# Eighteen spinning matmuls in three array shapes instead of twenty-six in one, ahead of a PE-bound encoder block

## The chip, the cores and the metric

The kernel runs on one core of one Trainium2 chip. The metric is device time in microseconds (us) of that core for one launch; lower is better. A core has five engines that run side by side and meet at semaphores: TensorE (PE, with its weight loads shown apart as PEld), VectorE (DVE), ScalarE (ACT), GpSimd (POOL) and SyncE (SP, which here only issues DMAs).

## The reference, cut to what matters

One encoder layer on 1024 tokens of width 1024: a projection, two kinds of attention, a gate, a second projection and a layer norm.

```python
h = jnp.einsum('bsd,de->bse', x, w_in[layer])
q_a, k_a, v_a, z_a, q_b, k_b, v_b, z_b = jnp.split(h, SPLIT_POINTS, axis=-1)
y_a = neighborhood_attention(q_a, k_a, v_a, rel_pos_bias[layer])      # 8 heads, 8 x 16 windows on a 16 x 64 grid
y_b = windowed_gqa_with_sink(rotary(q_b), rotary(k_b), v_b, sink_logits[layer])   # 8 heads, 2 key heads, |i-j| <= 128
mixed = jnp.concatenate([y_a * silu(z_a), y_b * silu(z_b)], axis=-1)
y = jnp.einsum('bse,ed->bsd', mixed, w_out[layer])
x = layer_norm(DEEPNORM_ALPHA * x + y, ln_gain[layer], ln_bias[layer])
```

None of this involves the spinning matmuls: they multiply zeros by zeros and nobody reads their result.

## The kernel before, in words

Precision is kept by splitting each float32 operand into a high and a low part and doing three matmuls (high by high, low by high, high by low) for each product. The kernel has these stages, in this order on PE:

1. **The spin** (line 412). A tile `warm` of 128 x 128 f16 zeros is written by DVE (line 127), and 26 matmuls multiply it by itself into one PSUM bank with the tag "t".
2. **The V projection, first half of the tokens** (`v_mms`, line 486). For each of eight slices k of the inner dimension there are 24 matmuls of 128 x 128 by 128 x 320: four token tiles, two column halves, three passes, in fp32r. For slice k the raw weights `wvraw` (DMA issued in line 435 or 457) become `wvh` on ACT (line 442, or 463 for the first slice) and `wvl` on DVE (line 445, or 466), and the raw tokens `xraw` (DMA in line 423 or 458) become `x` high (ACT, line 426, or DVE, line 464, for the first slice) and `x` low (line 429 or 465). The first matmul needs the first halves of `wvh` and of `x` high.
3. **The V projection, second half**, from f16 parts (line 486 again), which need scales worked out from all of x and wv.
4. **The combined projection** (`project`, line 379): 21 column tiles, with 16 x 3 matmuls of 128 x 512 each. From column tile 6 on, its matmuls are dealt out between those of the attention units (lines 816, 817, 881, 901).
5. **The output projection and the layer norm** (line 1031 and `final`), which end with the row tile 7 (lines 1104 to 1118).

The order of each engine's instructions is settled when the kernel is built, by a scheduler that runs the program against a timeline; inside `tc.manual_schedule()` it is the order of the text. DMAs of the first stages sit on SP's queue in the order in which the text issues them.

Tiles come from pools. `const` holds small tiles for the whole kernel; `vw` holds those of the V projection; the PSUM tag "t" has two banks that are handed out in turn.

The spin as it stands:

```python
warm = const.tile([128, 128], F16, name="warm")      # line 126
nc.vector.memset(warm, 0.0)
...
ps = bank("t")
for _ in range(26):
    nc.tensor.matmul(ps[:, :128], warm, warm, start=True, stop=True)     # line 412
```

Of the kernel before, what the change touches and what calls it, by code (L numbers as in the profile page):

```python
# [9 lines left out]
F16 = mybir.dt.float16  # L10
# [51 lines left out]
def hybrid_block(ctx, tc, xT, x, wt, wv, wo, bias, sink, gain, lbias, cos, sin, bmask, out):  # L62
    nc = tc.nc
    PS = bass.MemoryType.PSUM

    const = ctx.enter_context(tc.tile_pool(name="const", bufs=1))
# [7 lines left out]
    def bank(tag):  # L74
        bufs = {"pj": 2, "s": 4, "t": 2}[tag]
        return (ps1 if bufs == 1 else ps2).tile([128, 512], F32, tag=tag, name=f"ps_{tag}", bufs=bufs)
# [6 lines left out]
    def big_tile(name, shape=(128, 2, 512), dt=F32R):  # L83
        n = taken[0]
        taken[0] += 1
        tag = "big" if n < 8 or 16 <= n < 24 or n >= 32 + NS else "big2"
        return big.tile(list(shape), dt, tag=tag, name=name)

    xh, xl, x16h, x16l = {}, {}, {}, {}
    for half in range(2):  # L90
        for k in range(KT):
            t = big_tile(f"x{half}{k}", dt=F32 if half else F32R)
# [30 lines left out]
    sg = const.tile([128, 3], F32, name="sg")  # L123
    rsg = const.tile([128, 1], F32, name="rsg")
    junk = zp.tile([128, 2048], BF16, tag="ze", name="junk", bufs=1)
    warm = const.tile([128, 128], F16, name="warm")
    nc.vector.memset(warm, 0.0)
    ones = const.tile([128, 128], BF16, name="ones")
    nc.vector.memset(ones, 2.0 ** -13)
    bm = const.tile([128, 384], F32, name="bm")  # L130
    sk = const.tile([128, 8], F32, name="sk")
    nsk = const.tile([128, 8], F32, name="nsk")
# [272 lines left out]
    with ExitStack() as vctx:  # L405
        vp = vctx.enter_context(tc.tile_pool(name="vp", bufs=2))
        vw = vctx.enter_context(tc.tile_pool(name="vw", bufs=1))
        wvh, wvl = [], []
        wvm = vw.tile([128, KT], F32, name="wvm")
        ps = bank("t")  # L410
        for _ in range(26):
            nc.tensor.matmul(ps[:, :128], warm, warm, start=True, stop=True)  # L412

        wraw, xraw, nst = {}, {}, [0]

# [230 lines left out]
        for a in range(2):  # L646
            ps = bank(tags[4 + a])
# [211 lines left out]
    def quad(q):  # L859
        g, p, j, t, _ = units[4 * q]  # L860
        return g, p, j, t // 4 if g == "b" else t[0] // 2
# [319 lines left out]
    for i in range(-LD, NU + LO):  # L1181
# [38 lines left out]
        q, m = divmod(i - LP - 3, 4)  # L1220
        if i >= Q30 + 2:
            q, m = (NU // 4 - 2, i - Q30 - 2) if i < Q30 + 4 else divmod(i - LP - 3, 4)
        elif i >= Q30:
            q, m = -1, 0
# [10 lines left out]
        if 0 <= q < NU // 4:  # L1235
            g, p, j, h = quad(q)
# [88 lines left out]
```

## Time and profile before

| what | value |
|---|---|
| runs | 446.01, 446.91, 447.51 us; median 446.91 us |
| span of the profiled execution (first to last instruction) | 444.7 us |
| time of the profiled execution as a run | not listed; the runs lie 1.3 to 2.8 us above its span |
| PE busy | 437.5 us (98%), 3289 matmuls |
| DVE, ACT, POOL busy | 344.2, 308.3, 221.6 us |
| spin | from 0.98 us, 26 matmuls, 2.96 us |
| first matmul of the V projection | 3.89 us |

How to read it: the span starts with the first instruction on any engine, so times within the trace count from there. A matmul's end is modelled, and matmuls overlap, so the pace of PE is read from the distance between the starts of neighbours and not from their durations. The granted clock (PEclk) is the share of full speed that the throttle allows TensorE, as far as the profile recorded it.

### The profile page before, as it was taken

The page shows a single profiled execution, that of the slowest core. Times are in us where ns is not written, and L with a number is a line of the kernel's source. Part 1 is how long each engine was busy: PE and PEld are TensorE (multiplying, and loading weights), DVE is VectorE, ACT ScalarE, POOL GpSimd, SP SyncE. Part 2 cuts the span into 40 slices and gives each one's busy share as a digit, 9 for nine tenths or more (in the row PEclk, how much of TensorE's full clock was granted, in tenths as well). Part 3 has the DMA queues.
Part 4 walks back from the last instruction along what each step waited for, and adds up shares of the span by engine and source line. Part 5 has one row for each costly group of instructions (what it writes and reads, how often), then busy time and mean ns, then how long its engine had stood idle before and what let it go on. Part 6 is the DMA issues. An engine that isn't in the chain of part 4 may idle for free.

```text
span 444.7 us, 9505 instructions
## 1 busy us (share of the span) xinstructions
PE 437.5 (98%) x3289; PEld 255.5 (57%) x3289; DVE 344.2 (77%) x849; ACT 308.3 (69%) x700; POOL 221.6 (50%) x235
## 2 busy tenths in 40 slices
PE   9999999999999999999999999999999999999994
PEld 8997754444445565655565655656555654444453
DVE  5978967438986898887988888888878837589944
ACT  5759789766499988887868887888778946302401
POOL 0110074646839558866506767765574405205740
PEclk9999999999999999999999999999999999999997
DMA  8921469984659999587978899998999998103612
GB/s 272 390 91 60 145 235 339 336 292 169 213 127 214 206 190 181 98 162 143 164 127 175 169 182 180 213 170 213 192 204 253 167 172 347 55 0 102 232 69 72
DMA packets 133841, 81.39 MB, mean 183 GB/s; under 512 B 101280, under 2 KB 113440, under 8 KB 133536
## 3 DMA queue, kind: packets, MB, share of 16 engines
q1 hardware_dynamic: 133648, 80.64, 75.4%
q8 instruction: 26, 0.43, 0.4%
q14 instruction: 23, 0.19, 0.2%
q10 hardware_dynamic: 144, 0.13, 0.1%
HBM read 50.34 MB, written 9.96 MB: 136 GB/s over the span
## 4 chain that ended last, share of the span: by engine, by line
PE 91%; DMA 3%; POOL 3%; DVE 1%; issue 1%; ACT 1%; SPq 0%; POOLq 0%; DVEq 0%; ACTq 0%
PE ps_pj L379 44%; PE ps_s L1031 9%; PE ps_s L486 6%; PE ps_t L881 6%; PE ps_pj L1031 5%; PE ps_t L1031 5%; PE ps_s L816 4%; PE ps_s L817 4%; PE ps_pj L486 3%; PE ps_t L486 3%; DMA bias<-in_bias 3%; PE ps_t L901 1%; POOL wl L205 1%; PE ps_t L412 1%; POOL ks L295 1%
## 5 line engine op out<-in xcount | busy, mean ns | idle before, releaser
L379 PE MATMUL ps_pj<-xf,wh 128*128 128x512 f16 x672 | 202.1, 379 | 0.1
L379 PE MATMUL ps_pj<-xf,wl 128*128 128x512 f16 x336 | 127.3, 379 | 0.0
L379 PEld LDWEIGHTS <-wh 128*128 128x128 f16 x672 | 63.7, 98 | 60.4 <-DVE ks L263 0.5
L842 ACT ACTIVATE ps_s<-sn,nm 128x385 f32<-128x385 f32 (+3 forms) x128 | 70.1, 548 | 25.1 <-DVE nm L826 24.6
L853 DVE SCALAR_TENSOR_TENSOR split<-ps_s,split 128x384 f16<-128x384 f32 (+2 forms) x128 | 65.7, 513 | 27.5 <-ACT split L852 25.9
L1031 PEld LDWEIGHTS <-m 128*128 128x128 f16 x432 | 40.0, 98 | 41.1 <-DVE m L939 0.2
L852 ACT ACTIVATE split<-ps_s 128x384 f16<-128x384 f32 (+2 forms) x128 | 57.8, 452 | 2.5 <-DMA tr<-split 0.2
L204 POOL TENSOR_SCALAR wr<-wr,wsc 128x512 f32<-128x512 f32 x26 | 20.6, 791 | 68.1 <-ACT wh L199 61.6
L379 PEld LDWEIGHTS <-wl 128*128 128x128 f16 x336 | 32.9, 98 | 37.4
L826 DVE CUSTOM_DVE_ANT_0 sn<-ps_s,bm,nsk 128x384 f32<-128x384 f32 (+1 forms) x64 | 40.7, 636 | 2.0 <-PE ps_s L817 1.7
L1031 PE MATMUL ps_s<-wo,m 128*128 128x512 f16 (+1 forms) x192 | 40.8, 366 | 0.0
L816 PE MATMUL ps_s<-ks,qs 128*128 128x384 f16 (+4 forms) x128 | 39.2, 306 | 0.3 <-DVE qs L263 0.3
L817 PE MATMUL ps_s<-ks,qs 128*128 128x384 f16 (+4 forms) x128 | 39.2, 306 | 0.0
L826 DVE CUSTOM_DVE_ANT_0 sn<-ps_s,bias,sg 128x264 f32<-128x264 f32 (+1 forms) x64 | 35.0, 547 | 4.5 <-issue 1.5
L881 PEld LDWEIGHTS <-tr 128*128 128x128 f16 (+1 forms) x1104 | 36.6, 98 | 2.2
L205 POOL TENSOR_TENSOR wl<-wr,wh 128x512 f16<-128x512 f32 x26 | 32.7, 1257 | 2.2
L788 POOL TENSOR_SCALAR bias<-bias,rsg 128x552 f32<-128x552 f32 (+1 forms) x24 | 19.1, 797 | 23.8 <-DMA bias<-in_bias 22.6
L295 POOL COPY ks<-ks 64x512 f16<-64x512 f16 x40 | 26.0, 661 | 7.1 <-DVE ks L263 2.8
L1086 ACT ACTIVATE sd<-mv,eps 128x1 f32<-128x1 f32 x8 | 2.4, 295 | 36.5 <-DVE mv L1084 35.2
L1031 PE MATMUL ps_pj<-wo,m 128*128 128x512 f16 (+1 forms) x144 | 26.2, 326 | 0.0
L1130 POOL TENSOR_TENSOR xr<-xr,gb 128x512 f32<-128x512 f32 x7 | 9.8, 1396 | 32.4 <-ACT xr L1127 32.4
L842 ACT ACTIVATION_READ_ACCUMULATOR ps_s<-sn,nm 128x1 f32 x128 | 24.4, 190 | 0.0
(188 smaller groups left out, 813.8 us busy)
## 6 DMA issues: line engine op xcount, KB each, us to landing
ws<-in_wt SPq DMA_DIRECT2D x15, 512.0 KB, 5.9
wr<-in_wt SPq DMA_DIRECT2D x26, 256.0 KB, 3.6
wor<-in_wo SPq DMA_DIRECT2D x22, 256.0 KB, 3.5
bias<-in_bias SPq DMA_DIRECT2D x16, 276.0 KB, 3.3
xr<-in_x SPq DMA_DIRECT2D x8, 512.0 KB, 9.6
out<-xr SPq DMA_DIRECT2D x15, 256.0 KB, 2.1
bias<-in_bias SPq DMA_DIRECT2D x8, 368.0 KB, 3.8
wvraw<-in_wv SPq DMA_DIRECT2D x9, 320.0 KB, 5.8
```

The lines of the kernel that those rows point to most:

```text
L205: nc.gpsimd.tensor_sub(l, raw, h)
L295: nc.gpsimd.tensor_copy(t[o, sl], t[a, sl])
L379: nc.tensor.matmul(ps, a[:, k % 4, :], mv, start=(k == 0 and i == 0), stop=(k == KT - 1 and i == 2))
L486: nc.tensor.matmul(ps[:, :320], lh[:, ts], rh[:, cs], start=(k == ko[0] and i == 0), stop=(k == ko[-1] and i == 2))
L816: nc.tensor.matmul(ps[:, :m], q, sl[0], start=True, stop=False)
L817: nc.tensor.matmul(ps[:, :m], q, sl[1], start=False, stop=True)
L826: nc.vector.tensor_tensor_reduce(sn[:, :m], ps[:, :m], bias_t, sg[:, c:c + 1], init, op0=ALU.add, op1=ALU.min, accum_out=nm)
L842: nc.scalar.activation(pt[:, :m], sn[:, :m], AF.Exp, bias=nm, scale=-1.0, accum_out=sm[:, k:k + 1])
L852: nc.scalar.activation(hl[:, :m, 0, :c], src, AF.Copy, scale=PSCALE)
L853: nc.vector.scalar_tensor_tensor(hl[:, :m, 1, :c], src, PSCALE, hl[:, :m, 0, :c], op0=ALU.mult, op1=ALU.subtract)
L881: nc.tensor.matmul(ps[:, HD * m:HD * m + HD], a, b_, start=(i == 0), stop=(i == len(mms) - 1))
L1031: nc.tensor.matmul(ps, lh[:, ts], rh[:, cs], start=(e == EO[0] and i == 0), stop=(e == EO[-1] and i == 2))
```

## The change

`warm` moves from `const` to `vw` and grows to 128 x 256 f16; the memset of `ones` moves behind its memset. The spin takes a second "t" bank and runs five groups in the order of the text: 2 matmuls of 256 columns over the whole array, 6 of 128 columns that use 64 of the rows each (lower and upper half in turn, each half with a bank of its own), 2 of 128 columns over the whole array, 6 of 128 columns whose weights fill 64 of the array's columns each (in turn, into partitions 0 to 63 or 64 to 127 of one bank), and 2 of 256 columns over the whole array. Everything else is as it was, in the same order on every engine.

```diff
-    warm = const.tile([128, 128], F16, name="warm")
-    nc.vector.memset(warm, 0.0)
     ones = const.tile([128, 128], BF16, name="ones")
-    nc.vector.memset(ones, 2.0 ** -13)
...
-        ps = bank("t")
-        for _ in range(26):
-            nc.tensor.matmul(ps[:, :128], warm, warm, start=True, stop=True)
+        warm = vw.tile([128, 256], F16, name="warm")
+        nc.vector.memset(warm, 0.0)
+        nc.vector.memset(ones, 2.0 ** -13)
+        ps, ps_b = bank("t"), bank("t")
+
+        def spin(n, rows, cols, m=128):
+            for i in range(n):
+                j = i % 2
+                r = slice(64 * j, 64 * j + 64) if rows == 64 else slice(0, 128)
+                c = slice(64 * j, 64 * j + 64) if cols == 64 else slice(0, 128)
+                to = ps_b if rows == 64 and j else ps
+                nc.tensor.matmul(to[c, :m], warm[r, c], warm[r, :m], start=True, stop=True)
+
+        with tc.manual_schedule():
+            spin(2, 128, 128, 256)
+            spin(6, 64, 128)
+            spin(2, 128, 128)
+            spin(6, 128, 64)
+            spin(2, 128, 128, 256)
```

## The prediction

> **What bounds the kernel now.** I read the page's first two parts to see which engine holds the span and whether it ever lets go, then the timeline of the first 9 us, where the change sits, and then the stretches of the granted clock.
>
> ```profile
> span 444.7 us, 9505 instructions
> PE 437.5 (98%) x3289; PEld 255.5 (57%) x3289; DVE 344.2 (77%) x849; ACT 308.3 (69%) x700; POOL 221.6 (50%) x235
> PE   9999999999999999999999999999999999999994
> PEclk9999999999999999999999999999999999999997
> PE 91%; DMA 3%; POOL 3%; DVE 1%; issue 1%; ACT 1%; SPq 0%; POOLq 0%; DVEq 0%; ACTq 0%
> 0.00:100.00 100.00, 99.02 (x605) 69.39 (x606) 68.84 (x145) 75.42 (x141) 28.70 (x36) 1.00 0.71 240
> 100.00:200.00 100.00, 100.00 (x758) 53.84 (x757) 85.62 (x232) 80.30 (x195) 70.51 (x70) 1.00 0.81 173
> ```
>
> PE is busy for 437.5 of 444.7 us. In the first 100 us it is idle for 0.98 us (100.00 - 99.02), all of it ahead of the first spin, and in the next 100 us not at all. So whatever makes PE later in the first few microseconds makes the end later, and only what brings PE forward can run into a wait on something else. Now the start, row by row (start, duration, engine, line):
>
> ```profile
> 0.82 0.11 DVE L127 MEMSET warm<- 128x64 uint32 x1 [0.82 <-PEq L1314]
> 0.90 0.17 DVE L129 MEMSET ones<- 128x128 bf16 x1
> 0.98 2.96 PE L412 MATMUL ps_t<-warm 128*128 128x128 f16 x26 [0.98 <-DVE warm L127]
> 3.16 0.46 ACT L463 CAST wvh<-wvraw 128x320 fp32r<-128x320 f32 x1 [1.15 <-DMA wvraw<-in_wv]
> 3.45 0.29 DVE L464 CAST x<-xraw 128x256 fp32r<-128x256 f32 x1 [2.38 <-DMA xraw<-in_xT]
> 3.86 0.29 PEld L486 LDWEIGHTS ps_pj<-wvh,x 128*128 128x128 f32 x1 [0.18 <-ACT wvh L463]
> 3.89 0.61 PE L486 MATMUL ps_pj<-wvh,x 128*128 128x320 f32 x1
> 5.62 0.47 PE L486 MATMUL ps_t<-wvh,x 128*128 128x320 f32 x1
> 5.89 0.47 PE L486 MATMUL ps_s<-wvh,x 128*128 128x320 f32 x1
> 6.16 0.40 PE L486 MATMUL ps_t<-wvh,x 128*128 128x320 f32 x1
> 6.39 0.31 PE L486 MATMUL ps_s<-wvh,x 128*128 128x320 f32 x1
> 6.54 0.31 PE L486 MATMUL ps_t<-wvl,x 128*128 128x320 f32 x1
> 6.68 0.31 PE L486 MATMUL ps_s<-wvl,x 128*128 128x320 f32 x1
> 8.59 0.31 PE L486 MATMUL ps_pj<-wvh,x 128*128 128x320 f32 x1
> ```
>
> Three readings. First, the spin ends as the data comes: `x` is cast at 3.74 us (3.45 + 0.29), `wvh` at 3.62, and the first weight load of the V projection starts at 3.86. Second, equal matmuls start 0.27 us apart up to 6.16 and 0.147 us apart from 6.39 (6.39, 6.54, 6.68): PE runs at about half pace and then at full pace. Of the 0.23 us between 6.16 and 6.39, t at the old pace and the rest at the new give t/0.27 + (0.23 - t)/0.147 = 1, so t is 0.18 and the clock was **released at 6.34 us**, 5.36 us after the first spin. Third, this release isn't in the clock column:
>
> ```profile
> 3.00:4.00 1.00, 1.00 (x10) 0.82 (x8) 0.52 (x2) 0.46 (x1) 0.00 (x0) 1.00 0.69 197
> 4.00:5.00 1.00, 1.00 (x4) 1.00 (x5) 0.96 (x4) 0.00 (x0) 0.00 (x0) 1.00 1.04 329
> 439.75:440.00 0.25, 0.25 (x2) 0.22 (x1) 0.25 (x2) 0.00 (x0) 0.00 (x0) 0.66 0.00 0
> 440.00:440.25 0.25, 0.25 (x2) 0.00 (x0) 0.25 (x1) 0.00 (x0) 0.00 (x0) 0.50 0.00 0
> ```
>
> The clock column (third from the right) says 1.00 between 4 and 5 us, where the spacing says half: it shows no throttle before its first record. It does show the fall to 0.50 at the end; 0.66 in a quarter microsecond puts that fall at 439.83 us (0.68 of the quarter at half). So the kernel's first 5.4 us of PE work run at half pace, and the spin's only product is the moment of the release.
>
> **The change part by part.** The profiled execution's own time isn't listed; its span is 444.7 us and the median of the runs is 2.2 us more. I sum changes of the span and add them to the median of 446.91.
>
> *The start.* The memset of `warm` doubles to 128 x 256 f16. The nearest row is that of `ones`, 0.17 us against 0.11, so the spin starts at 1.04 in place of 0.98. DVE has nothing else until 3.45, so the later memset of `ones` is hidden there. On the path: 0.
>
> *The length of the spin.* The row of 26 gives 2.96 us with a modelled 0.31 for the last one:
>
> ```profile
> L412 PE MATMUL ps_t<-warm 128*128 128x128 f16 x26 | 3.0, 313 | 1.0 <-DVE warm L127 1.0
> ```
>
> so one of 128 columns takes (2.96 - 0.31)/25 = 0.106 us, and the last one has streamed in at 0.98 + 26 x 0.106 = 3.74. The new spin has 4 matmuls of 256 columns (0.85 us at twice the spacing), 2 of 128 over the whole array (0.21) and 12 over halves. No row of before shows a half array, so I take bounds: one after another, 12 x 0.106 = 1.27; in pairs side by side, half of it, 0.64. Between the groups the shape changes four times; each change costs between 0 (the next shape flows in behind) and 0.21 us (the modelled tail of one matmul, 0.313 - 0.106, has to run out first). Together 1.70 to 3.16 us, and the spin has streamed in between 2.74 and 4.20 us. I take one after another with half the tail, 2.33 + 0.42 = 2.75, ending at 3.79, since matmuls of this kind stand one after another in all rows of before. That is the old end within 0.05 us. At the late end the V projection would start up to 0.4 us later; the 0.4 us lost are at half pace, so they cost 0.4 x 0.147/0.27 = 0.2 us. At the early end PE stands idle for up to 1.0 us before 3.74, which costs nothing by itself, since the data isn't there.
>
> [...]
>
> *The release.* A microsecond more at half pace costs 1 - 0.147/0.27 = 0.45 us. If the monitor counts the new spin as it counted the old, the release stays. If the gaps and half-filled arrays count for less, the activity that it asks for is reached later. I take a release 0.4 us later, the middle of the idle time between 0.05 (one after another with half tails) and 0.9 (pairs, no tails): **+0.2 us**. From both sides: the latest release that rows give is that the whole spin counts for nothing, and the 5.36 us count from the first real matmul: 3.89 + 5.36 = 9.25, 2.91 us later, +1.3 us. The earliest can be bounded by data:
>
> ```profile
> 7.34 0.73 ACT L442 CAST wvh<-wvraw 128x640 fp32r<-128x640 f32 x1 [0.99 <-DMA wvraw<-in_wv]
> ```
>
> The second slice's `wvh` is cast at 8.07, after a wait of ACT for the DMA; with the lag of 0.12 between cast and load at the first matmul (3.74 to 3.86) its first matmul can't start before 8.19. It starts at 8.59. So even a clock that is full from the start saves at most **0.4 us**.
>
> *The rest.* 16 instructions fewer on PE (52 to 36) lie in the spin. On DVE, ACT, POOL and SP the order is the same, and no queue is passed. The second "t" bank shifts the turn of the two banks; the first new wait that it makes stands at the matmul of 5.62 (on a spin matmul that ended 1.5 us before or more): 0. Tiles behind `warm` in SBUF move by 256 bytes; no row prices an address, I take 0 and keep it as a rival.
>
> Sum: 0 + 0 + 0.2 = +0.2 us: 444.9 on the span, **447.1** on the median.
>
> **The rivals.**
>
> *A, the release comes a whole step later (slower).* The spin now ends sooner or counts less, so the monitor's check at which before was released finds too little. For it: the first microseconds show that some activity isn't enough (2 us of spin, 0.98 to 3, brought nothing), and 12 of 18 matmuls fill half an array. Against it: from 3.89 PE is dense whatever the spin does, and the last 2.4 us before 6.34 hold no spin at all. It decides when the idle or uncounted time before 3.86 exceeds what the check forgives. Price: release at 9.25, +1.3 us, and with a spin that also ends late, +1.5: 448.2 to 448.4; an execution of before that was released earlier than the profiled one loses more, up to 448.8 (the highest run of before, 447.51, and 1.3).
>
> [...]
>
> *B, the release comes earlier (slightly faster).* Two half-array matmuls side by side might count twice. For it: nothing in the rows. Price: -0.4 us by the bound above, 446.5; against a run whose release was later than the profiled one's it could be -1. It can hardly pass -0.3%.
>
> *C, the change doesn't act where it says.* Another layout in SBUF and of the banks, or an instruction fetch at another place, moves something in the 440 us behind. For it: the chain holds 3% of DMA and 3% of POOL, where PE stood only shortly late. Against it: PE's order is the same and its pace is set by its own columns. Either sign, 1 to 2 us.
>
> **How the numbers follow.** 0.3% of 446.91 is 1.34 us, about what a measurement of this kernel can tell from no change; so faster means under 445.57, slower over 448.25. Forecast (release moves by under a microsecond): 0.57, within. A: 0.25, of which 0.22 slower and 0.03 within. B: 0.09, of which 0.02 faster and 0.07 within. C: 0.09, of which 0.06 faster and 0.03 slower. Together faster 0.08, same 0.67, slower 0.25. The range takes in the early bound with the runs' own lower spread, and A whole: 445.6 (446.01 - 0.4) to 448.8.
>
> **What would show each step right or wrong.** The spin's row should start at 1.04 and its last matmul stream in by 3.8; an end under 3.4 says pairs ran side by side, one past 3.9 that the shape changes drain, and then the first matmul of the V projection moves from 3.89. The step in the spacing from 0.27 to 0.147 marks the release: near 6.3 to 6.8 the forecast holds, near 9 to 10 rival A, under 5.5 rival B, with ACT's cast of `wvh` as the next wait near 8.1. Since one execution is one draw of the release, the place of that step has to be read with the runs' spread. All rows behind 60 us should be shifted by one and the same amount; if the shift grows on the way, rival C is at work. The prediction would be wrong if the first matmuls of the V projection were slow for a reason other than the clock, or if the runs of before were typically released much later than the profiled one.

## The result, and the profile after

The changed kernel takes 447.88 us (median of 22 runs, 446.36 to 449.34) against 446.89 us before (22 runs, 445.49 to 448.79): a ratio of **1.0027, 95% interval 1.0016 to 1.0039**. It is slower, by some 1.2 us (0.0027 x 446.89; the two medians lie 1.0 us apart). The interval leaves out 1, and the ratio lies just inside the 0.3% that the forecast called "same". The forecast of 447.1 had the sign and a sixth of the size (0.2 of 1.2 us).

The page of the changed kernel, its span, PE line and the two rows of PE in slices (the profiled execution took 448.25 us, 1.85 us more than its span):

```profile
span 446.4 us, 9490 instructions
PE 437.8 (98%) x3281; PEld 254.3 (57%) x3281; DVE 345.1 (77%) x849; ACT 308.2 (69%) x700; POOL 221.6 (50%) x235
PE   8999999999999999999999999999999999999995
PEclk9999999999999999999999999999999999999999
```

PE's busy time is what it was (437.8 against 437.5); the first slice has lost a tenth. The clock column is no help, as before: it shows nine tenths or more from the first slice on. The timeline of the first microseconds (start, duration, engine, line; L418 is the spin, L499 the V projection):

```profile
0.83 0.17 DVE L408 MEMSET warm<- 128x128 uint32 x1 [0.83 <-PEq L1327]
1.05 2.37 PE L418 MATMUL ps_t<-warm 128*128 128x256 f16 x18 [1.05 <-DVE warm L408]
1.05 0.13 PEld L418 LDWEIGHTS <-warm 128*128 128x128 f16 x2 [1.05 <-DVE warm L408]
1.59 0.24 PEld L418 LDWEIGHTS <-warm 64*128 64x128 f16 x6 [0.41 <-issue]
2.03 0.13 PEld L418 LDWEIGHTS <-warm 128*128 128x128 f16 x2 [0.20 <-issue]
2.35 0.29 PEld L418 LDWEIGHTS <-warm 128*64 128x64 f16 x6 [0.20 <-issue]
2.81 0.13 PEld L418 LDWEIGHTS <-warm 128*128 128x128 f16 x2 [0.17 <-issue]
3.51 0.29 DVE L477 CAST x<-xraw 128x256 fp32r<-128x256 f32 x1 [2.37 <-DMA xraw<-in_xT]
3.95 0.60 PE L499 MATMUL ps_pj<-wvh,x 128*128 128x320 f32 x1 [0.53 <-DVE x L477]
7.02 0.47 PE L499 MATMUL ps_s<-wvl,x 128*128 128x320 f32 x1
7.29 0.44 PE L499 MATMUL ps_pj<-wvh,x 128*128 128x320 f32 x1
7.55 0.32 PE L499 MATMUL ps_s<-wvh,x 128*128 128x320 f32 x1
7.71 0.31 PE L499 MATMUL ps_pj<-wvh,x 128*128 128x320 f32 x1
9.18 0.31 PE L499 MATMUL ps_pj<-wvh,x 128*128 128x320 f32 x1
```

Three things are to be seen. The spin is short: 2.37 us with the modelled tail of its last matmul (0.42), so that one starts at 3.00 and has streamed in near 3.21. Ahead of the first real matmul stands a gap: the row of 3.95 has an idle time of 0.53 us by modelled ends, 0.74 us by streaming (3.95 - 3.21), where before had 0.15 (3.89 - 3.74). And the spacing steps from 0.27 to 0.15 us near 7.56, not 6.34: the release is 1.22 us later in this execution. The second slice's first matmul moves from 8.59 to 9.18 us.

One trace isn't enough for the rest. The same matmul (by its place in PE's order) starts 0.59 us later than before everywhere from 8 to 240 us, and then falls back further: 0.95 us at 273, 2.35 at 318, 2.57 at 365, 2.46 at the last matmul, of which the tail gives back some. The views of PE's waits, of the changed kernel and of two kernels told below, the late spin and the early spin of 16:

```profile
PE ps_t L894 <- DMA tr<-split: 1.1, 2, 0.7
PE ps_pj L376 <- DVE ks L260: 0.3, 1, 0.3
```

```profile
PE ps_t L890 <- DMA tr<-split: 0.5, 2, 0.3
PE ps_pj L376 <- DVE ks L260: 0.3, 1, 0.3
```

```profile
PE ps_pj L495 <- DVE x L473: 1.0, 1, 1.0
PE ps_pj L376 <- DVE ks L260: 0.3, 1, 0.3
```

The columns are total, times and longest. PE waits here and there for a transposing DMA behind 240 us. These waits come and go from one trace to the next, whether the release is early or late: the late spin has them although its release came early, the kernel with the short gap, told below, has one of 0.7 us near 317 us with its release at 4.95, and the early spin of 16 has the latest release of all twelve traces and no such DMA wait. I put them to the scatter of single executions, not to the change, and judge the change by medians and by the first 60 us. Each kernel has one trace, so this is argued and not shown.

### The profile page after: what moved, and what is told of

Its sections match the earlier page's. It is cut to its first block, busy times and chain, and to the rows that moved or that the text cites. A ratio compares the mean times of both kernels' runs of the same rounds, so it can differ in the third digit from the quotient of the medians.

```text
span 446.4 us, 9490 instructions
## 1 busy us (share of the span) xinstructions
PE 437.8 (98%) x3281; PEld 254.3 (57%) x3281; DVE 345.1 (77%) x849; ACT 308.2 (69%) x700; POOL 221.6 (50%) x235
## 4 chain that ended last, share of the span: by engine, by line
PE 92%; POOL 2%; DVE 2%; DMA 1%; issue 1%; ACT 1%; SPq 0%; POOLq 0%; ACTq 0%
PE ps_pj L376 45%; PE ps_s L1044 9%; PE ps_t L894 7%; PE ps_s L499 6%; PE ps_pj L1044 5%; PE ps_t L1044 5%; PE ps_s L829 4%; PE ps_s L830 4%; PE ps_pj L499 3%; PE ps_t L499 3%; PE ps_t L914 1%; DMA bias<-in_bias 1%; POOL ks L292 1%; POOL wl L202 1%; DMA xraw<-in_xT 1%
```

## The experiments

All kernels start from the changed one and alter only what the diff shows. The price of a later release is the prediction's 0.45 us per us. "Gapless run" means the stretch of PE work without a long gap in which the release falls.

**1. The old spin in the new place.**

```diff
-            spin(2, 128, 128, 256)
-            spin(6, 64, 128)
-            spin(2, 128, 128)
-            spin(6, 128, 64)
-            spin(2, 128, 128, 256)
+            spin(26, 128, 128)
```

> The changed kernel's tile, pool, banks and text order, with the 26 whole-array matmuls of 128 columns again. Three theories. IDLE: the monitor counts the time in which PE is busy, and the spin that ends 0.53 us early leaves a gap that makes a check fail. SHAPE: half-array matmuls count for less than whole ones. ELSEWHERE: the new place of the tile, the second bank or the fixed order moves something later in the kernel. IDLE and SHAPE expect a ratio to before of 1.000 (0.999 to 1.001); ELSEWHERE expects 1.0027, as the change gave.

Measured: 446.80 us, ratio 1.000 (0.9985 to 1.0015). The tile's pool, the second bank and the fixed order cost nothing that can be seen: ELSEWHERE falls.

**2. A spin as short as the change's, of whole arrays only.**

```diff
-            spin(6, 64, 128)
-            spin(2, 128, 128)
-            spin(6, 128, 64)
+            spin(12, 128, 128)
```

> As the change, but the 12 matmuls over halves and the 2 between them become 12 of 128 columns over the whole array: 4 x 0.212 + 12 x 0.106 = 2.12 us of streaming, so the spin ends near 3.2 us as in the change, and PE has the same gap ahead of the first real matmul, without half arrays and without changes of shape. IDLE expects the loss of the change, a ratio of 1.002 to 1.003. SHAPE expects at most the gap's own 0.5 us x 0.45 = 0.24 us, 1.000 to 1.001. ELSEWHERE expects 1.0027.

Measured: 447.51 us, 1.0020 (1.0006 to 1.0034). The loss is there without a single half array. Its timeline, with the gap and the step:

```profile
1.05 2.31 PE L418 MATMUL ps_t<-warm 128*128 128x256 f16 x16 [1.05 <-DVE warm L408]
3.93 0.61 PE L497 MATMUL ps_pj<-wvh,x 128*128 128x320 f32 x1 [0.56 <-DVE x L475]
8.07 0.47 PE L497 MATMUL ps_s<-wvh,x 128*128 128x320 f32 x1
8.34 0.37 PE L497 MATMUL ps_pj<-wvl,x 128*128 128x320 f32 x1
8.54 0.31 PE L497 MATMUL ps_s<-wvl,x 128*128 128x320 f32 x1
```

The release is at 8.46 us, behind a gap of 0.78 us (its last matmul of 256 columns starts at 1.05 + 2.31 - 0.42 = 2.94 and has streamed in at 3.15).

**3. The change's spin, with its gap filled.**

```diff
             spin(2, 128, 128, 256)
+            spin(5, 128, 128)
```

> The spin of the change, with 5 more matmuls of 128 columns over the whole array behind it (5 x 0.106 = 0.53 us), which fill the gap ahead of the first real matmul; the half-array groups stay. IDLE expects the loss gone, 1.000 (0.999 to 1.001). SHAPE expects a good part of the loss left, 1.001 to 1.0027. ELSEWHERE expects 1.0027. First real matmul at 3.9 to 4.0 us in all three.

Measured: 446.49 us, 0.9998 (0.9983 to 1.0012). All half arrays and shape changes are still there, and the loss is gone:

```profile
1.05 2.90 PE L418 MATMUL ps_t<-warm 128*128 128x256 f16 x23 [1.05 <-DVE warm L408]
3.89 0.60 PE L500 MATMUL ps_pj<-wvh,x 128*128 128x320 f32 x1
6.43 0.47 PE L500 MATMUL ps_s<-wvh,x 128*128 128x320 f32 x1
6.69 0.42 PE L500 MATMUL ps_t<-wvl,x 128*128 128x320 f32 x1
6.95 0.32 PE L500 MATMUL ps_s<-wvl,x 128*128 128x320 f32 x1
```

With 1 and 2 this puts the loss on the short spin and not on the shape. The filled spin has more matmuls as well as no gap; which of the two counts is left to experiments 5, 9 and 10.

**4. No spin at all.**

```diff
-            spin(2, 128, 128, 256)
...
-            spin(2, 128, 128, 256)
+            spin(0, 128, 128)
```

> The change without any spinning matmul (the tile is still written). This is the most that a useless spin can cost: the activity starts at 3.95 us instead of 0.98, 2.97 us later, x 0.45 = 1.34 us, a ratio of 1.0030 (1.002 to 1.004) by IDLE and by SHAPE alike; ELSEWHERE has no number of its own, and would be shown by a ratio near 1.000 or above 1.005.

Measured: 448.76 us, 1.0047 (1.0032 to 1.0063), with the release at 9.15 us in its trace. That is more than the 1.0030 expected, by a hair outside the interval. The change, with 18 spinning matmuls, lost between half and all of what a spin is worth.

**5. The idle time ahead of the spin instead of behind it.**

```diff
-        warm = vw.tile([128, 256], F16, name="warm")
+        warm = vw.tile([128, 1024], F16, name="warm")
...
-            spin(2, 128, 128, 256)
...
-            spin(2, 128, 128, 256)
+            spin(21, 128, 128)
```

> The idle time moved from behind the spin to ahead of it: the tile is 128 x 1024, so that its memset takes about 0.58 us (0.17 for 128 columns of words, four times the columns) and the spin starts near 1.46 us; 21 whole-array matmuls of 128 columns (21 x 0.106 = 2.23 us) then last to about 3.7 us. That is about the busy time of the short whole-array spin, but without its gap. GAPLESS (the release needs one whole stretch of the monitor without a gap, so only the start of the last gapless run counts): the run starts 0.48 us later than before, x 0.45 = 0.22 us, a ratio of 1.0005 (0.9995 to 1.0015). AMOUNT (the release needs so much busy time, gaps or not): the loss of the short whole-array spin, 1.0020 (1.001 to 1.003).

Measured: 446.92 us, 1.0019 (1.0008 to 1.0029). By the ratio this speaks for AMOUNT and against GAPLESS, whose 1.0005 lies outside. Its trace has the release at 5.48 us, 2.98 us earlier than the short whole-array spin with nearly the same number of columns. The rows of the spin and of the step:

```profile
1.45 2.42 PE L418 MATMUL ps_t<-warm 128*128 128x128 f16 x21 [1.45 <-DVE warm L408]
5.15 0.46 PE L495 MATMUL ps_pj<-wvl,x 128*128 128x320 f32 x1
5.42 0.35 PE L495 MATMUL ps_s<-wvl,x 128*128 128x320 f32 x1
5.60 0.31 PE L495 MATMUL ps_t<-wvh,x 128*128 128x320 f32 x1
```

So time and trace disagreed, and experiments 9 and 10 repeat the contrast with a larger difference.

**6. A short gap.**

```diff
-            spin(2, 128, 128, 256)
...
-            spin(2, 128, 128, 256)
+            spin(23, 128, 128)
```

> 23 whole-array matmuls of 128 columns in place of 26, from 1.05 to about 3.51 us, so that a gap of 0.4 us stands ahead of the first real matmul at 3.9. GAPLESS with a strict bound: as without a spin, +1.3 us, 1.0030 (1.002 to 1.004). GAPLESS with a bound that forgives 0.4 us in a stretch: 1.000 (0.999 to 1.001). AMOUNT: 0.4 x 0.45 = 0.2 us, 1.0004, which this run can't tell from the second.

Measured: 446.82 us, 1.0009 (0.9996 to 1.0023); the strict bound (1.0030) falls. The trace:

```profile
1.05 2.63 PE L418 MATMUL ps_t<-warm 128*128 128x128 f16 x23 [1.05 <-DVE warm L408]
3.84 0.61 PE L495 MATMUL ps_pj<-wvh,x 128*128 128x320 f32 x1 [0.15 <-DVE x L473]
4.78 0.39 PE L495 MATMUL ps_s<-wvh,x 128*128 128x320 f32 x1
5.01 0.31 PE L495 MATMUL ps_pj<-wvl,x 128*128 128x320 f32 x1
```

The spin streams in at 1.05 + 23 x 0.106 = 3.49, the gap is 0.35 us, and the release comes at 4.95, only 1.1 us behind it: a gap of 0.35 us was forgiven.

**7. Half arrays only.**

```diff
-            spin(2, 128, 128, 256)
...
-            spin(2, 128, 128, 256)
+            spin(50, 64, 128)
```

> 50 matmuls over 64 rows each, lower and upper half in turn, nothing else in the spin: 25 pairs at 0.106 us a pair are 2.65 us, from 1.05 to about 3.7 us. IDLE (shape doesn't count): 1.000 (0.999 to 1.001). SHAPE (half an array counts for half): no stretch that holds the spin passes, so as without a spin, 1.003 (1.002 to 1.004).

Measured: 446.69 us, 1.0008 (0.9995 to 1.0020); SHAPE's 1.003 falls. The trace:

```profile
1.05 2.85 PE L418 MATMUL ps_t<-warm 64*128 64x128 f16 x50 [1.05 <-DVE warm L408]
4.02 0.61 PE L495 MATMUL ps_pj<-wvh,x 128*128 128x320 f32 x1
4.42 0.35 PE L495 MATMUL ps_s<-wvh,x 128*128 128x320 f32 x1
4.61 0.31 PE L495 MATMUL ps_pj<-wvh,x 128*128 128x320 f32 x1
```

50 half-array matmuls take the time of 25 whole ones (24 x 0.106 + 0.31 = 2.85 us), so pairs do run side by side. The clock is released at 4.50 us with 2.65 us of such pairs, a gap of 0.32 us and 0.48 us of real matmuls behind it. That is 3.45 us behind the first of them, the shortest such time of the twelve traces in the table below; spins of whole arrays alone, without a long gap, took 3.52 to 5.86. So the traces give no sign that a pair counts for less than a whole matmul. A half array that runs without its partner wasn't tried.

**8. A pure delay of PE.**

```diff
             ps = new_group()
+            for _ in range(22 if n == 0 and half == 0 else 0):
+                nc.tensor.matmul(ps[:, :128], ones, ones, start=True, stop=True)
             for k in range(KT):
```

(with the 26 whole-array matmuls of experiment 1 as the spin)

> The 26 whole-array matmuls as in the first experiment, and 22 more of 128 columns at the start of the combined projection near 59 us, where the clock has long been full: about 22 x 0.057 = 1.25 us of pure delay of PE with no part in the release. ONE-TO-ONE (a delay of PE is passed on as it is): +1.25 us, 1.0028 (1.0018 to 1.0038). AMPLIFIED (in the trace without a spin a shift of 1.28 us behind the release became 4.4 us at the end): +2.5 us or more, 1.0055 and up. ABSORBED: under 1.001.

Measured: 448.02 us, 1.0027 (1.0006 to 1.0048): 1.2 us for 22 matmuls, one to one within a wide interval. The trace says it sharper, with the row of the 22:

```profile
58.59 1.39 PE L361 MATMUL ps_pj<-ones 128*128 128x128 bf16 x22
```

Against before, the same matmul stands 0.79 us earlier up to 57 us (its release came at 4.57), 0.44 us later from 60 us on, a step of 1.23 us, and 0.44 us later still at 430 us. AMPLIFIED finds no support: this delay doesn't grow, and the trace of experiment 9, 1.37 us behind before at 20 us, is 1.91 behind at 400. But PE was never more than 0.44 us behind before here, so the growth from 1.28 to 4.4 us in the trace without a spin stays unexplained.

**9. An early spin of 16, and 10. the same 16 late.**

```diff
-            spin(2, 128, 128, 256)
...
-            spin(2, 128, 128, 256)
+            spin(16, 128, 128)
```

and, in the tenth alone,

```diff
-        nc.vector.memset(warm, 0.0)
+        with tc.manual_schedule():
+            nc.vector.memset(junk, 0.0)
+            nc.vector.memset(warm, 0.0)
```

> 16 whole-array matmuls of 128 columns from 1.05 to about 2.75 us (16 x 0.106 = 1.70 us), then a gap of some 1.1 us to the first real matmul near 3.9. GAPLESS with a bound that forgives a gap of about 0.4 us but not one of 0.75: as the change and as without a spin, some +1.2 us, a ratio of 1.0027 (1.0017 to 1.0037), and in the trace a release not before about 6.8 us. AMOUNT (busy time adds up over gaps): 1.1 x 0.45 = 0.5 us, 1.0011, and the same as in the next kernel.

> The same 16 whole-array matmuls, but late: a memset of another tile of 128 x 1024 words goes ahead on VectorE (four times that of 0.17 us or more, about 0.9 us), so that the spin runs from about 2.05 to 3.75 us and leaves no gap to speak of. GAPLESS: only the start of the run counts, 2.05 in place of 0.98, 1.07 x 0.45 = 0.5 us at most, a ratio of 1.0008 (0.9998 to 1.0018), about 0.8 us less than the kernel before it in this list; a release not before about 5 us. AMOUNT: the same loss as that kernel, 1.0011.

Measured: early 447.83 us, 1.0026 (1.0013 to 1.0038); late 446.89 us, 1.0013 (0.9997 to 1.0030), 0.94 us apart by medians for the same 16 matmuls, where GAPLESS expected 0.8 and AMOUNT 0. The ratios alone overlap; the traces don't. Early, then late:

```profile
1.05 1.89 PE L418 MATMUL ps_t<-warm 128*128 128x128 f16 x16 [1.05 <-DVE warm L408]
3.97 0.60 PE L495 MATMUL ps_pj<-wvh,x 128*128 128x320 f32 x1 [1.03 <-DVE x L473]
8.91 0.47 PE L495 MATMUL ps_t<-wvh,x 128*128 128x320 f32 x1
9.18 0.36 PE L495 MATMUL ps_s<-wvh,x 128*128 128x320 f32 x1
9.38 0.31 PE L495 MATMUL ps_t<-wvh,x 128*128 128x320 f32 x1
```

```profile
2.13 1.89 PE L420 MATMUL ps_t<-warm 128*128 128x128 f16 x16 [2.13 <-DVE warm L410]
3.94 0.61 PE L497 MATMUL ps_pj<-wvh,x 128*128 128x320 f32 x1
6.48 0.45 PE L497 MATMUL ps_s<-wvh,x 128*128 128x320 f32 x1
6.75 0.33 PE L497 MATMUL ps_t<-wvl,x 128*128 128x320 f32 x1
6.92 0.31 PE L497 MATMUL ps_s<-wvl,x 128*128 128x320 f32 x1
```

Early, PE was still at half pace at 9.18 us, after 1.7 us of spin and 5.2 us of dense work, 6.9 us in all; late it was released at 6.78 after 4.65 us. In experiment 7 it was released after 3.45. More busy time with a long gap in it did not do what less without one did: AMOUNT falls. The scatter of the release doesn't save it: the 6.9 us lie outside the 3.45 to 5.87 us after which the eight kernels of the table below that spin without a long gap were released.

All twelve traces together, with the release worked out from the step in the spacing, as in the prediction, and read to 0.01 us from the trace's clock record, whose first entry starts there:

| kernel | gapless run starts | release | between |
|---|---|---|---|
| half arrays only | 1.05 | 4.50 | 3.45 |
| pure delay | 1.05 | 4.57 | 3.52 |
| gap of 0.35 us | 1.05 | 4.95 | 3.90 |
| late spin of 21 | 1.45 | 5.48 | 4.03 |
| before | 0.98 | 6.34 | 5.36 |
| late spin of 16 | 2.13 | 6.78 | 4.65 |
| old spin, new place | 1.05 | 6.91 | 5.86 |
| gap filled | 1.05 | 6.92 | 5.87 |
| **the change** (gap 0.74) | 3.95 | 7.56 | 3.61 |
| short whole spin (gap 0.78) | 3.93 | 8.46 | 4.53 |
| no spin | 3.89 | 9.15 | 5.26 |
| early spin of 16 (gap 1.2) | 3.97 | 9.29 | 5.32 |

Counted from the start of the gapless run, every release falls between 3.45 and 5.87 us; counted from the first spin, the change and the early spins would have taken 6.5 to 8.2. The same spin of 26 from 1.05 us, released at 4.57 in experiment 8 and at 6.91 in experiment 1, shows that the time differs from one execution to the next, here by 2.34 us. In all twelve traces full speed then lasts for 433.49 or 436.91 us, two values 3.41 us apart by the clock records of before and of the change (433.493 and 436.906); why there are two, and what sets the moment of a release within the 3.45 to 5.87 us, no run here shows.

From the first spin, the kernel with the gap of 0.35 us was released after 3.90 us, inside the 3.45 to 5.87 of the other seven that spin without a long gap; those with gaps of 0.74, 0.78 and 1.2 us were released after 6.51, 7.41 and 8.24, outside it. The ratios agree: 1.0009 (0.9996 to 1.0023) with the gap of 0.35 us, 1.0027, 1.0020 and 1.0026 with the longer ones, all three with intervals above 1. What is forgiven thus ends between 0.35 and 0.74 us in these kernels.

## Why the prediction was right or wrong

- **What bounds the kernel** held. PE's early loss goes through to the end: the pure delay of 1.23 us at 59 us is still 1.23 us at 430.
- **The start** held to 0.01 us (1.05, with the memset at 0.17).
- **The length of the spin** was mis-sized: 3.21 us for its end in place of 3.79. The halves run in pairs: from the row of 1.59 to that of 2.03 six of them and one change of shape take 0.44 us, where one after another they alone would take 0.64. Pairs were the other bound. A change of shape costs 0.12 us on average (2.16 us from 1.05 to 3.21, less 1.70 of streaming, over four changes), a little over half of my upper bound. Pairs with that bound at all four changes would have ended at 3.57 (1.04 + 1.70 + 4 x 0.207). PEld is idle for 0.17 to 0.20 us at the last three changes.
- **The release** is the step that failed. I priced the gap as time that is merely added, "a release 0.4 us later, +0.2 us". The gap of 0.74 us did not add its own length; the release came as if the run counted afresh from behind it: from 3.95 in place of 0.98. If the time from the start of a run to its release is the same on average, that makes the release 2.97 us later, 1.3 us by the price of 0.45, as an estimate from these two starts; 1.2 were measured. The price and the direction were right. That the range held the time isn't the forecast's merit, since it took in rival A whole, and the ratio stayed inside "same" by 0.1 us, which is luck. The release of 0.4 us was also loosely drawn: the middle of its 0.05 and 0.9 is 0.48, which gives the same +0.2.
- **Rival A** was what happened, with its price (+1.3) and its condition, "when the idle or uncounted time before 3.86 exceeds what the check forgives". The experiments put that point between 0.35 us (1.0009) and 0.74 (1.0027). A check or a monitor as such is in no trace; the traces show when the spacing steps. The release of this trace, 7.56, lies between the places that I had named for the forecast and for A: it is one draw. A's other half, that half arrays might count less, finds no support in experiments 3 and 7. I gave it 0.25 because I had taken the late end of the spin for likelier than the early one, and because the argument against it, dense work from 3.89 on, overlooked that 6.34 is only 2.45 us behind 3.89, where no trace has a release less than 3.45 us behind the start of such a run.
- **Rival B** and its bound of 0.4 us: the traces of the short gap and of the half arrays, released at 4.95 and 4.50, stand 0.39 and 0.41 us ahead of before at 20 us, just at the bound, but the one released at 4.57 gained 0.79. The bound rested on when the data of one execution came. It didn't matter to the result.
- **Rival C** fell with experiment 1, by the ratio. By the sign that I had named, a shift that grows on the way, the trace of the change speaks for it (0.59 us at 240, 2.57 at 365); but experiment 1 has the tile, the banks and the order of the change, and its shift stays (0.25 us at 10, 0.29 at 430). That sign was a poor one, since traces with an early release grow too: the one of the short gap goes from 0.39 us ahead of before at 20 us to 0.51 behind at 320.
- **The spread of the runs.** The releases found lie up to 2.4 us apart for kernels with the same start (3.45 to 5.87 us behind it), 1.1 us by the price. The 22 runs of before spread over 3.3 us, so the moment of the release isn't all of it, and that the first three spanned 1.5 us was chance.

Open: where between 0.35 and 0.74 us the bound lies. The loss without a spin (1.0047) is larger than the 1.0030 of the estimate, and the late spin of 21 (1.0019) lost more than its 0.5 us later start explains; their intervals miss the estimated values narrowly, two of ten comparisons, and I found no mechanism. What sets off the DMA waits behind 240 us in some executions wasn't tried. No kernel here beats the one before: filling the gap brings the change back to it, and a spin that starts sooner would need its tile sooner than 0.93 us.

## What to carry to other kernels

The spin that is to release TensorE's clock had to last here until the first real matmul, to within 0.35 us; its length in time mattered, not its shape or the number of its matmuls (50 over halves 1.0008, 26 over the whole array 1.000, 16 whole ones that end 0.78 us early 1.0020), and when it is short the end should be kept, not the start (16 late cost 0.9 us less than 16 early). Price such a gap as a step, not a slope: here 0.35 us of idle time cost nothing that can be seen (1.0009, 0.9996 to 1.0023), and 0.74 us cost between half and all of what the spin is worth. When work is moved onto parts of the array, ask how it runs beside itself, since pairs take half the time (50 half-array matmuls in the 2.85 us of 25 whole ones) and leave the gap. And read the throttle ahead of the first clock record from the spacing of equal matmuls (0.27 us against 0.15 here, with the clock column at 1.00 on both sides of the step).

## What the runs showed of the hardware

- Half-array matmuls on the two halves of the rows start within 0.01 us of each other and run side by side (50 in 2.85 us). With a spin of such pairs the clock was released 3.45 us behind its start, with whole arrays alone, without a long gap, 3.52 to 5.86.
- A change between whole, half-row and half-column shapes costs 0.12 us on average at half pace.
- Equal matmuls start 0.27 us apart up to the release and 0.15 us apart from it on. Full speed then lasted for 433.49 or 436.91 us in all twelve traces.
- With a gap of 0.35 us behind the spin the release came 3.90 us from its start, with gaps of 0.74, 0.78 and 1.2 us 6.51, 7.41 and 8.24 us from it.
- Releases came between 4.50 and 9.29 us into the span. For kernels that start alike they differed by up to 2.4 us (4.50 to 6.92), which is 1.1 us of time at 0.45 us per us.
